# Longer rows for the split weights: eight buffers at eight places modulo 256 bytes

## The chip, the cores and the metric

The kernel runs on one core of a Trainium2 chip. The metric is the device time of one execution in microseconds (us), lower is better. The core has the engines PE (TensorE, the matrix unit; its weight loads are listed apart as PEld), ACT (ScalarE), DVE (VectorE), POOL (GpSimd) and SP (SyncE, used here to issue DMAs). SBUF is the on-chip memory with 128 partitions; a "place" below is the byte address of a row within a partition, taken modulo 256.

## The reference, cut to what matters

One layer of a hybrid decoder trunk on 512 tokens plus 16 meta tokens, 1024 channels wide, in float32:

```python
u = rmsnorm(h, mix_norm_w[i])
proj = u @ w_in[i]
...
y_pool = pool_mixer(u_pool, pool_w_group[i], pool_scale[i]) @ w_pool_up[i]
y_ssd = mamba2_branch(z, xbc, dt_raw, ...) @ w_ssd_out[i]
h = h + (gate_pool * y_pool + gate_ssd * y_ssd) @ w_o[i]
v = rmsnorm(h, mlp_norm_w[i])
hid = jax.nn.relu(v @ w_ff1[i])
h = h + (hid * hid) @ w_ff2[i]
...
out = rmsnorm(h, final_norm_w)
return out[:, N_META:]
```

Nearly all of the work is matrix products with weights that are read once from DRAM.

## The kernel before, in words

Each float32 factor of a large product is split into a high part (type fp32r, a copy by ACT) and a low part (what is left, a subtraction by DVE). A product then takes three matmuls: high by high, high by low, low by high. The weights come in 171 blocks of 128 partitions by 1024 columns, in the order of use, each by one DMA on SP's queue.

The buffers. The pool `wp` (L55) holds three raw buffers (tag `raw`), four buffers for high parts (tag `whi`) and four for low parts (tag `wlo`), each with rows of 4096 bytes, used in turn. `block_tiles` (L63) takes one of each kind; `block_part` (L70) issues the DMA, the cast `whi<-raw` (L73) and the subtraction `wlo<-raw,whi` (L74). `split` (L713) does the same from a tile that is already there (L717, L718, names `shi` and `slo`), and takes its buffers from the same tags. Tiles begin at multiples of 32 bytes. In the program as built the raw buffers begin at bytes 14816, 18912 and 23008, the high ones at 27104, 31200, 35296 and 39392, the low ones at 43488, 47584, 51680 and 55776: all eleven at place 224 modulo 256. The pool of the normed input follows: a pad of 64 bytes (`u_pad`, L124), then `uh` and `ul` (L125, L126) with rows of 2304 bytes, of which the 16 meta tokens begin at place 224 and the 512 others at place 32. Most other fp32r tiles (`yh`, `yl`, `vh`, `vl`, `hh`, `hl`, the factors of the output projection) begin at place 224 too; the pooled parts `ph`, `pl` begin at 32. The matrix of ones `ones_r` (L97), stationary at L486 and L487, begins at 128.

Who reads the split weights, and how. A matmul has a stationary operand (loaded by PEld, 128 columns of 512 bytes) and a moving one (streamed through, up to 512 columns).

- `proj_step` (L139; matmuls at L143, L144, L146): the weights are stationary, the input moves: `uh` or `ul`. In the "wide" form (`px`, `pp`) the 528 tokens go in two runs of 264, 260 or 258 columns, so places 224 and 0, or 0 and 16, or 16 and 24; in the "narrow" form (`pz`, `pgp`, `pgs`) 512 columns begin at place 32. High weights go twice (with `uh`, `ul`), low ones once.
- `mm3` (L88; L90, L91, L92): the weights are stationary, `yh`/`yl`, `yph`/`ypl` or `vh`/`vl` move, 512 columns at place 224 (tiles `pso`, `psp`, `psl`, `pup`, `pf`), or `ph`/`pl` at place 32 (`pg`).
- `wo_prod` (L771 to L773), `prod` (L956 to L958) and the last chunk (L1057): here the split weights move, 512 columns (256 at the very end), and the other factor (`hh`, `hl` and the like) is stationary. In each group of three the moving row is high, low, high.

A column slice of a block begins a multiple of 512 bytes into its row, so it has the place of its row. The order of the work is the order in which the program is written, per engine; waits come from the tile framework, by tile. `weave` (L503) interleaves the steps of two generators.

Of the kernel before, what the change touches and what calls it, by code (L numbers as in the profile page):

```python
# [10 lines left out]
F32R = mybir.dt.float32r  # L11
# [3 lines left out]
P = 128  # L15
# [34 lines left out]
def kernel(ctx: ExitStack, tc, xT, x, w, vec, fnw, out):  # L50
# [4 lines left out]
    wp = ctx.enter_context(tc.tile_pool(name="wp", bufs=4, side="left"))  # L55
# [4 lines left out]

    nblk = [0]

    def block_tiles():  # L63
        b = nblk[0]
        nblk[0] += 1
        return (b, wp.tile([P, 1024], F32, tag="raw", name=f"raw{b}", bufs=3),
                wp.tile([P, 1024], F32R, tag="whi", name=f"whi{b}"),
                wp.tile([P, 1024], F32R, tag="wlo", name=f"wlo{b}"))

    def block_part(t, c):  # L70
        b, raw, hi, lo = t
# [4 lines left out]
    def block():  # L76
        t = block_tiles()
        block_part(t, slice(0, 1024))
        return t[2:]
# [98 lines left out]
    runsB, viewB = wide(pB)  # L178

    wdt, wB = block_tiles(), block_tiles()  # L180
    b, raw, hi, lo = wdt
    nc.sync.dma_start(raw[:, :256], w[b, :, :256])
# [528 lines left out]
        woq[name, i] = t  # L711

    def split(src):  # L713
        hi = wp.tile([P, 1024], F32R, tag="whi", name=f"shi{nsplit[0]}")
        lo = wp.tile([P, 1024], F32R, tag="wlo", name=f"slo{nsplit[0]}")
        nsplit[0] += 1
        act.copy(hi, src)  # L717
        dve.tensor_tensor(lo, src, hi.bitcast(F32), op=ALU.subtract)  # L718
        return hi, lo

    nsplit = [0]
# [7 lines left out]
    for n, d in enumerate(MERGE):  # L729
        if n < len(WO_ORDER):  # L730
            wo_load(*WO_ORDER[n])
        if n + 1 < NK:
            gts.append(gate_ssd(MERGE[n + 1]))
        if n >= NK - 2:
            first.append(split(woq["b11", n - NK + 2]))
        ps = psum2(f"pup{d}")[:, :SEQ]
        wh, wl = block()
        for i, k in enumerate(ks):
            c = slice(k * P, (k + 1) * P)
            mm3(ps, (wh[:, c], wl[:, c]), yps[k], i == 0, i == NK - 1)  # L740
        dve.tensor_tensor(acc[d], acc[d], gts[n], op=ALU.mult)
        dve.tensor_tensor(m1[d], m1[d], ps, op=ALU.mult)
        dve.tensor_tensor(acc[d], acc[d], m1[d], op=ALU.add)
        factors(d)
# [70 lines left out]
    def wo_split(name):  # L815
        return [split(woq[name, i]) for i in range(2)]
# [186 lines left out]
    for c in range(NC - 1):  # L1003
        b11, b12, b22, b21 = (quarter(n) for n in ("b11_", "b12_", "b22_", "b21_"))
        z, e = c == 0, c == NC - 2
        prod(av, c, A11, split(b11), True, False)
        onto(0, 0, alpha, ADD)
        t1 = sum_of(b11, b12, "", b11)
        t2 = sum_of(t1, b22, f"t2_{c}")
        filler()  # L1010
        prod(av, c, S2, split(t2), False, False)
        onto(0, 1, alpha, SUB)
        filler()
        prod(av, c, S3, split(sum_of(b12, b22, "", b12)), False, False)
        onto(1, 1, alpha, SUB)
        filler()
        prod(av, c, A22, split(sum_of(t2, b21, "", t2)), False, True)
        onto(1, 0, alpha, ADD)
        if e:
            prod(q5v, c, S1, split(t1), z, True)  # L1020
            for t in range(2):
                onto(0, 1, q5v[t], ADD, t)
                onto(1, 1, q5v[t], ADD, t)
        elif c < NC - 3:
            filler()
        prod(av, c, S4, split(b22), True, True)
        onto(0, 1, alpha, ADD)
        prod(p2v, c, A12, split(b21), z, False)
        if not e:
            prod(q5v, c, S1, split(t1), z, False)  # L1030
# [9 lines left out]
    for t in range(4):  # L1040
        T, st = t // 2, slice((t % 2) * P, (t % 2 + 1) * P)
        n = 0
        for half in range(2):
            parts = [(0, 512)] if half == 0 or t < 3 else [(0, 256), (256, 256)]
            for a, m in parts:
# [4 lines left out]
                for k, seg in ((1, (A11, 3)[T]), (0, (A12, A22)[T])):  # L1050
                    wh, wl = wq[k, half]
                    for p in range(2):
                        x0 = p * 512 + a
                        f = i == 0 and not (T == 0 and half == 0)
# [152 lines left out]
```

## Time and profile before

| | |
|---|---|
| time, median of 2 runs | 1025.45 us (1025.28 to 1025.62) |
| span of the profiled execution, first to last instruction | 1023.3 us |
| what the median has beside that span | 2.15 us |
| granted TensorE clock, mean | 0.999 |

The page gives no other time for the profiled execution than its span, so the profile's numbers are put against 1023.3 us, and 2.15 us are added to reach the median. In a group's row "xcount | busy, mean ns of one" the mean of a matmul is its length from start to end; matmuls overlap, so the next one starts long before that. What a matmul costs is read from the distance between the starts of successive rows of the timeline.

### The profile page before, as it was taken

The numbers are of one execution on the slowest core, as the hardware profiler recorded it, in microseconds if no ns is written. First come the engines' busy times: TensorE is split into PE (matmuls) and PEld (weight loads), VectorE is DVE, ScalarE is ACT, GpSimd is POOL, SyncE is SP. The second block draws the span as 40 slices with busy tenths as digits, with TensorE's granted clock in tenths as the row PEclk, the third lists the DMA queues.
The fourth block names the chain that finished last, engine by engine and source line by source line (L and its number), as shares of the span: only waits on it lengthen the run. The fifth ranks groups of instructions, "written<-read, shape, count | busy, mean of one in ns | idle before, by whom it ended". The sixth has DMA issues, their size and how long they took to land.

```text
span 1023.3 us, 14063 instructions
## 1 busy us (share of the span) xinstructions
PE 1014.6 (99%) x5697; PEld 876.7 (86%) x5697; DVE 730.3 (71%) x954; ACT 552.5 (54%) x728; POOL 88.7 (9%) x52
## 2 busy tenths in 40 slices
PE   9999999999999999999999999999999999999997
PEld 8889989998879898988899888888888888888886
DVE  7978788687746586978755457975777577666866
ACT  7775968586627339573244343474545355454444
POOL 0100000000000000000000001003040421413400
PEclk9999999999999999999999999999999999999999
DMA  7243051414332331414532333224323323334112
GB/s 237 72 160 103 21 166 38 148 46 141 102 101 86 103 104 42 145 41 141 189 102 84 103 104 120 86 91 156 103 69 122 120 83 113 95 102 124 42 42 83
DMA packets 29281, 105.63 MB, mean 103 GB/s; under 512 B 3296, under 2 KB 4256, under 8 KB 28192
## 3 DMA queue, kind: packets, MB, share of 16 engines
q1 hardware_dynamic: 26496, 92.75, 28.7%
q0 software_dynamic: 2000, 11.08, 3.0%
q8 instruction: 45, 0.74, 0.3%
q10 hardware_dynamic: 720, 0.91, 0.3%
q14 instruction: 20, 0.16, 0.1%
HBM read 102.55 MB, written 2.16 MB: 102 GB/s over the span
## 4 chain that ended last, share of the span: by engine, by line
PE 96%; DVE 2%; ACT 0%; DMA 0%; issue 0%; SPq 0%; ACTq 0%
PE px L143 6%; PE px L144 6%; PE pf L92 6%; PE pf L91 6%; PE px L146 6%; PE pf L90 6%; PE alpha L956 3%; PE alpha L957 3%; PE alpha L958 3%; PE pz L143 3%; PE pz L146 3%; PE pz L144 3%; PE py L470 2%; PE pso L90 2%; PE pp L144 2%; PE pp L146 2%
## 5 line engine op out<-in xcount | busy, mean ns | idle before, releaser
L73 ACT CAST whi<-raw 128x1024 fp32r<-128x1024 f32 (+1 forms) x131 | 135.7, 1043 | 220.0 <-PE pf L91 55.8
L74 DVE TENSOR_TENSOR wlo<-raw,whi 128x1024 fp32r<-128x1024 f32 (+1 forms) x131 | 163.6, 1251 | 112.6 <-ACT whi L73 105.3
L143 PE MATMUL px<-uh,whi 128*128 128x264 f32 (+1 forms) x448 | 121.2, 290 | 0.7 <-DVE ct L334 0.7
L144 PE MATMUL px<-ul,whi 128*128 128x264 f32 (+1 forms) x448 | 118.9, 285 | 0.0
L90 PE MATMUL pf<-vh,whi 128*128 128x512 f32 x256 | 99.8, 390 | 0.0
L92 PE MATMUL pf<-vh,wlo 128*128 128x512 f32 x256 | 99.6, 389 | 0.0
L91 PE MATMUL pf<-vl,whi 128*128 128x512 f32 x256 | 99.6, 389 | 0.0
L146 PE MATMUL px<-uh,wlo 128*128 128x264 f32 (+1 forms) x448 | 90.8, 284 | 0.0
L143 PEld LDWEIGHTS px<-uh,whi 128*128 128x128 f32 x448 | 84.6, 189 | 2.8 <-issue 2.6
L144 PEld LDWEIGHTS px<-ul,whi 128*128 128x128 f32 x448 | 84.8, 189 | 0.3
L718 DVE TENSOR_TENSOR slo<-b,shi 128x1024 fp32r<-128x1024 f32 x35 | 49.1, 1403 | 31.6 <-ACT shi L717 31.6
L146 PEld LDWEIGHTS px<-uh,wlo 128*128 128x128 f32 x448 | 69.4, 188 | 0.3 <-issue 0.3
L717 ACT CAST shi<-b 128x1024 fp32r<-128x1024 f32 x35 | 36.8, 1050 | 47.2 <-PE pf L91 36.4
L91 PEld LDWEIGHTS pf<-vl,whi 128*128 128x128 f32 x256 | 48.1, 188 | 10.0
L90 PEld LDWEIGHTS pf<-vh,whi 128*128 128x128 f32 x256 | 48.1, 188 | 9.9
L92 PEld LDWEIGHTS pf<-vh,wlo 128*128 128x128 f32 x256 | 48.1, 188 | 9.9
L967 POOL TENSOR_TENSOR b<-b,b 128x1024 f32<-128x1024 f32 x14 | 35.7, 2548 | 238.3 <-DVE slo L718 238.3
L956 PE MATMUL alpha<-shi,hh 128*128 128x512 f32 x140 | 54.6, 390 | 0.0
L957 PE MATMUL alpha<-slo,hh 128*128 128x512 f32 x140 | 54.5, 389 | 0.0
L958 PE MATMUL alpha<-shi,hl 128*128 128x512 f32 x140 | 54.5, 389 | 0.0
L783 DVE TENSOR_TENSOR ht<-ht,alpha 128x1024 f32<-128x1024 f32 x35 | 42.5, 1214 | 10.9 <-PE alpha L958 10.9
L143 PE MATMUL pz<-uh,whi 128*128 128x512 f32 x112 | 44.0, 393 | 0.0
(412 smaller groups left out, 2513.7 us busy)
## 6 DMA issues: line engine op xcount, KB each, us to landing
raw<-in_w SPq DMA_DIRECT2D x129, 512.0 KB, 3.6
b<-in_w SPq DMA_DIRECT2D x28, 512.0 KB, 3.6
abc<-acs_d POOLq DMA_DIRECT2D x8, 1024.0 KB, 7.2
wob<-in_w SPq DMA_DIRECT2D x8, 512.0 KB, 4.6
xt<-in_xT SPq DMA_DIRECT2D x8, 264.0 KB, 5.6
ht<-in_x POOLq DMA_DIRECT2D x4, 512.0 KB, 6.7
w<-in_w SPq DMA_DIRECT2D x4, 512.0 KB, 3.6
out_dram<-out SPq DMA_DIRECT2D x4, 320.0 KB, 2.4
```

What stands on the lines that cost most here:

```text
L73: act.copy(hi[:, c], raw[:, c])
L74: dve.tensor_tensor(lo[:, c], raw[:, c], hi[:, c].bitcast(F32), op=ALU.subtract)
L90: pe.matmul(ps, ah, bh, start=first, stop=False)
L91: pe.matmul(ps, ah, bl, start=False, stop=False)
L92: pe.matmul(ps, al, bh, start=False, stop=last)
L143: pe.matmul(o, wh, rhs[0][k][:, c], start=k == 0, stop=False)
L144: pe.matmul(o, wh, rhs[1][k][:, c], start=False, stop=False)
L146: pe.matmul(o, wl, rhs[0][k][:, c], start=False, stop=k == NK - 1)
L718: dve.tensor_tensor(lo, src, hi.bitcast(F32), op=ALU.subtract)
L956: pe.matmul(ps[t], a[0], wh[:, cs], start=f, stop=False, skip_group_check=True)
L957: pe.matmul(ps[t], a[0], wl[:, cs], start=False, stop=False, skip_group_check=True)
L958: pe.matmul(ps[t], a[1], wh[:, cs], start=False, stop=l, skip_group_check=True)
```

## The change

Each high and low buffer is allocated with 1032 columns instead of 1024, 4128 bytes instead of 4096, and the first 1024 are used. 4128 is 16 times 256 plus 32, so each next buffer begins 32 bytes further on modulo 256: the four high ones at places 224, 0, 32 and 64, the four low ones at 96, 128, 160 and 192. The raw buffers stay. Everything that is allocated behind these eight moves up by 8 times 32, which is 256 bytes, and keeps its place. A high buffer and the low buffer of the same block differ by 128 bytes in place.

```diff
+    def half_tile(tag, name):
+        return wp.tile([P, 1024 + 8], F32R, tag=tag, name=name)[:, :1024]
+
     def block_tiles():
         b = nblk[0]
         nblk[0] += 1
         return (b, wp.tile([P, 1024], F32, tag="raw", name=f"raw{b}", bufs=3),
-                wp.tile([P, 1024], F32R, tag="whi", name=f"whi{b}"),
-                wp.tile([P, 1024], F32R, tag="wlo", name=f"wlo{b}"))
+                half_tile("whi", f"whi{b}"), half_tile("wlo", f"wlo{b}"))
...
     def split(src):
-        hi = wp.tile([P, 1024], F32R, tag="whi", name=f"shi{nsplit[0]}")
-        lo = wp.tile([P, 1024], F32R, tag="wlo", name=f"slo{nsplit[0]}")
+        hi = half_tile("whi", f"shi{nsplit[0]}")
+        lo = half_tile("wlo", f"slo{nsplit[0]}")
```

## The prediction

> **What bounds the kernel now.** I read the page first: its head, the slices, the chain that ended last.
>
> ```profile
> span 1023.3 us, 14063 instructions
> PE 1014.6 (99%) x5697; PEld 876.7 (86%) x5697; DVE 730.3 (71%) x954; ACT 552.5 (54%) x728; POOL 88.7 (9%) x52
> PEclk9999999999999999999999999999999999999999
> PE 96%; DVE 2%; ACT 0%; DMA 0%; issue 0%; SPq 0%; ACTq 0%
> ```
>
> PE is busy for 99% of the span at the full granted clock and is 96% of the chain. So the time is the sum of the distances between starts of successive matmuls, and little else. The engines that write the buffers whose rows get longer come next, from the groups by line:
>
> ```profile
> L73 ACT CAST whi<-raw 128x1024 fp32r<-128x1024 f32 (+1 forms) x131 | 135.7, 1043 | 220.0 <-PE pf L91 55.8
> L74 DVE TENSOR_TENSOR wlo<-raw,whi 128x1024 fp32r<-128x1024 f32 (+1 forms) x131 | 163.6, 1251 | 112.6 <-ACT whi L73 105.3
> ```
>
> The cast waits for PE to free a buffer (L91 and others), not PE for the cast: the weights arrive ahead of their use.
>
> What one matmul costs depends on its form, and here the timeline of PE is read, first rows and last rows of undisturbed stretches. First 512 columns whose moving row begins at place 224: six rows of the product with the squared hidden layer, then the next projection.
>
> ```profile
> 786.76 0.39 PE L956 MATMUL alpha<-shi,hh 128*128 128x512 f32 x1
> 786.99 0.39 PE L957 MATMUL alpha<-slo,hh 128*128 128x512 f32 x1
> 787.22 0.39 PE L958 MATMUL alpha<-shi,hl 128*128 128x512 f32 x1
> ...
> 793.11 0.39 PE L91 MATMUL pf<-vl,whi 128*128 128x512 f32 x1
> 793.34 0.39 PE L92 MATMUL pf<-vh,wlo 128*128 128x512 f32 x1
> 793.56 0.39 PE L956 MATMUL alpha<-shi,hh 128*128 128x512 f32 x1
> ```
>
> From 786.76 to 793.56 there are 30 distances: 226.7 ns each, the same in `alpha`, where split weights move, and in `pf`, where they are stationary. Now 512 columns at place 32, a narrow projection between two products `pup` at 224:
>
> ```profile
> 585.04 0.40 PE L143 MATMUL pgs<-uh,whi 128*128 128x512 f32 x1
> ...
> 585.74 0.39 PE L143 MATMUL pgs<-uh,whi 128*128 128x512 f32 x1
> ...
> 590.32 0.39 PE L146 MATMUL pgs<-uh,wlo 128*128 128x512 f32 x1
> 590.55 0.40 PE L90 MATMUL pup<-yph,whi 128*128 128x512 f32 x1
> ...
> 592.86 0.39 PE L91 MATMUL pup<-ypl,whi 128*128 128x512 f32 x1
> ...
> 595.81 0.39 PE L92 MATMUL pup<-yph,wlo 128*128 128x512 f32 x1
> ```
>
> The projection settles: 585.74 to 590.55 is 21 distances of 229.0 ns, so place 32 costs 2.3 ns more than place 224. The first three take 233 ns each (0.70 us), 4 more. Behind the change of place back to 224 the first ten take 231 ns each (2.31 us), and only then, from 592.86 to 595.81, the 13 distances are 226.9. So the place of a moving row is seen in the time, and after a change PE needs up to ten matmuls to get back into its best step. That is the whole stage on which this change acts.
>
> **The change, part by part.** It adds no instruction, no DMA and no wait, and moves none past another. It moves addresses. Four things can come of that.
>
> 1. The cast and the subtraction write rows at other places. They do the same work; I price that at nothing. The cover is the wait quoted above (ACT idle 220.0 us ahead of L73). If each became a tenth dearer, some 105 ns a cast, PE would still not wait, except for the first blocks; ACT has 0% of the chain and DVE 2%, so a tenth of all of DVE's share, about 2 us, is a bound that lies far above.
>
> 2. The split weights as moving rows, 864 matmuls: 588 at L956 to L958, 168 at L771 to L773, 108 at L1057. Counted from these groups and their smaller ones:
>
> ```profile
> L956 PE MATMUL alpha<-shi,hh 128*128 128x512 f32 x140 | 54.6, 390 | 0.0
> L957 PE MATMUL alpha<-slo,hh 128*128 128x512 f32 x140 | 54.5, 389 | 0.0
> L958 PE MATMUL alpha<-shi,hl 128*128 128x512 f32 x140 | 54.5, 389 | 0.0
> ```
>
> They now begin at place 224 without exception; afterwards one buffer in eight does, so 756 matmuls are moved off it. The price of another place is known from one row, place 32: +2.3 ns. Bounds: at the least -6.7 ns (worked out under the third rival), at the most +4.3 ns, what the unsettled rows behind the change of place show. I take +2.3, the one settled value: 756 x 2.3 = 1.7 us.
>
> 3. In these 864 the place also changes within each group of three (high, low, high: two changes, 128 bytes apart), 576 changes. What does a change cost when it comes steadily? The wide projections change place four times in six matmuls. These rows are 264 columns at 224 and 0 in turn, and 258 columns at 16 and 24:
>
> ```profile
> 113.32 0.28 PE L143 MATMUL px<-uh,whi 128*128 128x264 f32 x1
> ...
> 116.99 0.28 PE L143 MATMUL px<-uh,whi 128*128 128x264 f32 x1
> 121.46 0.28 PE L143 MATMUL px<-uh,whi 128*128 128x258 f32 x1
> ...
> 124.34 0.28 PE L143 MATMUL px<-uh,whi 128*128 128x258 f32 x1
> ```
>
> 30 distances of 122.3 and 24 of 120.0 ns. From 258 to 512 columns at 226.7 is 0.42 ns a column; by that 264 columns would be 122.5 with no change of place at all. So the steady change costs nothing here. The other end is the change into `pgs`: three distances together 0.70 us instead of 0.687, 13 to 16 ns a change, 576 x 16 = 9.2 us. I take 1.5 ns, near the rows that alternate steadily as these will: 0.9 us.
>
> 4. The split weights as stationary operand: 4128 matmuls (L90 to L92 464 each, L143 to L146 912 each), whose weight rows now come from eight places. All of them begin at 224 now, but the sums over heads load a matrix of ones from place 128:
>
> ```profile
> L486 PEld LDWEIGHTS png<-qhg,ones_r 128*128 128x128 f32 x8 | 1.5, 188 | 0.3
> L90 PEld LDWEIGHTS pf<-vh,whi 128*128 128x128 f32 x256 | 48.1, 188 | 9.9
> ```
>
> 188 ns from both, and the load lies beside the matmul ahead of it. I take zero for the place of a stationary row, with eight loads as evidence. The upper bound is the first rival, the lower one the fourth.
>
> **Weighed against the skill.** The rows above say that the moving row's place counts. The Trainium skill (SBUF — State Buffer, "Who interferes with whom") says that PE has two read ports, one for the moving operand and one for LDWEIGHTS, independent of each other, and that "PE and ACT never wait on anyone". The equal 188 ns agree with it; the 229.0 against 226.7 ns show that a place has a price all the same. By that page alone, the change would be worth zero, which is the second rival.
>
> Sum: 1.7 + 0.9 = 2.6 us on the span of 1023.3, so 1025.9. The median has 2.15 us beside the span (1025.45 less 1023.3), which nothing here touches: 1028.0 us.
>
> **The rivals.**
>
> First, the step is lost everywhere. If the distance hangs on how the moving and the stationary row lie to each other, then high and low weights that differ by 128 bytes change that relation inside each group of three, and PE stays in the unsettled state: 231 ns instead of 226.7 for the 512-column matmuls at 224 (1344 with stationary weights and the 864 above), 231 instead of 229.0 for 816 at place 32, and perhaps 1 ns for 1920 wide ones. 2208 x 4.3 + 816 x 2.0 + 1.9 us = 13.0 us, so 1038.5. For it: the unsettled rows exist and last ten matmuls although nothing waits. Against it: the equal load times, and the steady alternation at 120.0 ns.
>
> Second, nothing happens: the place matters only in `uh`-like rows, or settles by itself: 1025.4 us. For it: 256, 258, 264 columns lie on one line. Against it: 229.0 ns at place 32, also for another tensor.
>
> Third, a little faster. The distance may grow in steps: 258 columns take 120.0, and the last products, of 256 columns at place 224, take the same, 20 distances in 2.40 us:
>
> ```profile
> 1014.69 0.28 PE L1057 MATMUL pl<-shi,hh 128*128 128x256 f32 x1
> ...
> 1017.09 0.28 PE L1057 MATMUL last<-shi,hl 128*128 128x256 f32 x1
> ```
>
> If a step is 16 columns (6.7 ns at 0.42 each) and a row that begins at a multiple of 64 bytes saves one, half of the 864 gain: 432 x -6.7 = -2.9, the other places +0.7, so about 1023.2 us. Against it: no row here shows place 0, 64, 128 or 192 with 512 columns.
>
> Fourth, far faster. At 0.42 ns a column 512 columns are worth 215.1 ns; 11.6 ns of each distance are left over. If half of that were a clash of equal places and went, 4992 x 5.8 = 29 us, 996 us. The Trainium skill (TensorE: Matmul & The Clock Gate, "Back-to-back issue gap") gives N/2.4 + 2.5, an estimate of 216 ns for 512, as what can be reached; the trace has 226.7. Against this rival: 258 columns at 16 and 24, clear of the weights' place, have the same surplus.
>
> Fifth, slower by more than 2%: some of the new pairs of places cost PE one whole step of 6.7 ns in every matmul, at all 4992 of fp32r with split weights: 33 us, 1059 us. It decides from 4.1 ns a matmul on (20.5 us over 4992). For it: place 32 costs something at each matmul. Against it: even the unsettled rows average only 4.3 ns over the best.
>
> **How the numbers follow.** Forecast 0.46 (1028.0; its own range 1025 to 1036, by the bounds of terms 2 and 3), step lost everywhere 0.24 (1038.5), nothing 0.13 (1025.4), a little faster 0.10 (1023.2), slower by over 2% 0.05, far faster 0.02. For eight in ten I leave out the far cases and the dear end of the first rival: 1022.5 to 1040. Two per cent is 20.5 us, and the chances go by that although the two runs shown lie within 0.4 us of each other, so that a smaller difference can be told too: faster 0.02, same 0.93, slower 0.05.
>
> **What would show it.** Timeline of PE in the changed kernel: `pf` rows still 226.7 apart, `pgs` 229.0 and `px` 122.3 (term 4 right); `alpha` rows on average some 3 ns further apart, differing from buffer to buffer (terms 2 and 3). If `pf` rows lie 229 to 232 apart, the first rival holds; if `alpha` rows from some buffers are 220 apart, the third. Casts and subtractions stay at 1043 and 1251 ns. The forecast falls if the place of a stationary row has a price: it is the term with the most matmuls and the thinnest evidence.

## The result and the profile after

The changed kernel takes 1037.46 us (1037.43 to 1037.49, 2 runs) against 1025.45 before: ratio 1.0118, interval 1.0089 to 1.0147, slower by 12.0 us. That lies inside the range on record, and beside its number: 1038.5 was the first rival, 1028.0 the forecast. It is under the two per cent (20.5 us) from which the prediction speaks of slower, but far more than the 0.4 us between the two runs of the kernel before.

The page of the changed kernel (two lines were added ahead of all matmuls, so L90 is now L92, L143 is L145 and L956 is L958):

```profile
span 1035.4 us, 14063 instructions
PE 1027.2 (99%) x5697; PEld 878.5 (85%) x5697; DVE 730.0 (71%) x954; ACT 553.0 (53%) x728; POOL 88.9 (9%) x52
PEclk9999999999999999999999999999999999999999
PE 99%; DVE 1%; ACT 0%; issue 0%; ACTq 0%
L75 ACT CAST whi<-raw 128x1024 fp32r<-128x1024 f32 (+1 forms) x131 | 135.4, 1040 | 226.3 <-PE pf L93 58.2
L76 DVE TENSOR_TENSOR wlo<-raw,whi 128x1024 fp32r<-128x1024 f32 (+1 forms) x131 | 163.1, 1247 | 116.9 <-ACT whi L75 116.9
```

The span grew by 12.1 us and PE's busy time by 12.6, with the same number of matmuls at the same clock. Casts and subtractions kept their length (1040 and 1247 ns, before 1043 and 1251), and ACT waits longer for PE than before. No wait was added: PE takes longer over the same list.

The timeline of PE shows where, at the same matmuls as before. First the six of `alpha` and the 24 of `pf`; then a narrow projection (its high weights at place 64) and the product `pup` behind it; then the wide runs:

```profile
793.91 0.39 PE L958 MATMUL alpha<-shi,hh 128*128 128x512 f32 x1
...
800.87 0.40 PE L958 MATMUL alpha<-shi,hh 128*128 128x512 f32 x1
588.99 0.40 PE L145 MATMUL pgs<-uh,whi 128*128 128x512 f32 x1
...
593.89 0.39 PE L92 MATMUL pup<-yph,whi 128*128 128x512 f32 x1
...
599.22 0.40 PE L94 MATMUL pup<-yph,wlo 128*128 128x512 f32 x1
113.74 0.29 PE L145 MATMUL px<-uh,whi 128*128 128x264 f32 x1
...
117.39 0.28 PE L145 MATMUL px<-uh,whi 128*128 128x264 f32 x1
121.86 0.28 PE L145 MATMUL px<-uh,whi 128*128 128x258 f32 x1
...
124.76 0.28 PE L145 MATMUL px<-uh,whi 128*128 128x258 f32 x1
```

30 distances from 793.91 take 232.0 ns each (before 226.7), 21 from 588.99 take 233.3 (229.0), the 23 of `pup` 231.7, and there is no settled stretch at 226.9 behind its tenth row any more. The wide runs barely move: 121.7 and 120.8 ns (122.3 and 120.0).

Both traces hold the same matmuls in the same order, so every distance can be set against its own. Added up by use, the differences are:

| matmuls | count | longer by, us |
|---|---|---|
| stationary weights, moving row at 224 (`pf`, `pso`, `psp`, `psl`, `pup`) | 1344 | 6.0 |
| split weights moving (`alpha` and its like, `wo_prod`, last chunk) | 864 | 4.1 |
| stationary weights, moving row at 32 (narrow, `pg`) | 816 | 2.2 |
| stationary weights, wide | 1920 | -0.1 |
| all others | 753 | -0.1 |

Two thirds of the loss (6.0 and 2.2 us) sit where the moving rows stayed at the same place and only the stationary ones went elsewhere.

### The profile page after: what moved, and what is told of

Read it like the earlier page. It is cut to its first block, busy times and chain, and to the rows that moved or that the text cites. A ratio compares the mean times of both kernels' runs of the same rounds, so it can differ in the third digit from the quotient of the medians.

```text
span 1035.4 us, 14063 instructions
## 1 busy us (share of the span) xinstructions
PE 1027.2 (99%) x5697; PEld 878.5 (85%) x5697; DVE 730.0 (71%) x954; ACT 553.0 (53%) x728; POOL 88.9 (9%) x52
## 4 chain that ended last, share of the span: by engine, by line
PE 99%; DVE 1%; ACT 0%; issue 0%; ACTq 0%
PE px L145 6%; PE px L148 6%; PE px L146 6%; PE pf L94 6%; PE pf L92 6%; PE pf L93 6%; PE alpha L960 3%; PE alpha L958 3%; PE alpha L959 3%; PE pz L148 3%; PE pz L146 3%; PE pz L145 3%; PE py L472 2%; PE pso L92 2%; PE pp L148 1%; PE pp L145 1%
## 5 line engine op out<-in xcount | busy, mean ns | idle before, releaser
L75 ACT CAST whi<-raw 128x1024 fp32r<-128x1024 f32 (+1 forms) x131 | 135.4, 1040 | 226.3 <-PE pf L93 58.2
L76 DVE TENSOR_TENSOR wlo<-raw,whi 128x1024 fp32r<-128x1024 f32 (+1 forms) x131 | 163.1, 1247 | 116.9 <-ACT whi L75 116.9
L145 PE MATMUL px<-uh,whi 128*128 128x264 f32 (+1 forms) x448 | 121.2, 291 | 0.7 <-DVE ct L336 0.7
L92 PE MATMUL pf<-vh,whi 128*128 128x512 f32 x256 | 101.0, 395 | 0.0
L145 PEld LDWEIGHTS px<-uh,whi 128*128 128x128 f32 x448 | 84.5, 189 | 2.8 <-issue 2.6
L92 PEld LDWEIGHTS pf<-vh,whi 128*128 128x128 f32 x256 | 48.3, 189 | 10.8
L958 PE MATMUL alpha<-shi,hh 128*128 128x512 f32 x140 | 55.3, 395 | 0.0
L148 PE MATMUL pz<-uh,wlo 128*128 128x512 f32 x112 | 44.3, 395 | 0.0
```

What stands on the lines that cost most here:

```text
L75: act.copy(hi[:, c], raw[:, c])
L76: dve.tensor_tensor(lo[:, c], raw[:, c], hi[:, c].bitcast(F32), op=ALU.subtract)
L92: pe.matmul(ps, ah, bh, start=first, stop=False)
L145: pe.matmul(o, wh, rhs[0][k][:, c], start=k == 0, stop=False)
L148: pe.matmul(o, wl, rhs[0][k][:, c], start=False, stop=k == NK - 1)
L958: pe.matmul(ps[t], a[0], wh[:, cs], start=f, stop=False, skip_group_check=True)
```

## The experiments

Two theories were set against each other. R, the relation: the distance between matmuls depends on the place of the moving row less that of the stationary row, modulo 256. A, the alternation: what costs is that high and low weights of one group of three lie 128 bytes apart, which keeps PE from settling. All runs start from the kernel before; padding is written as tiles that nothing uses, always 256 bytes in all (512 with four places), so that what lies behind keeps its place. In the diffs, `...` stands for lines left out.

**All eight buffers at place 32.**

```diff
...
+        raw = wp.tile([P, 1024], F32, tag="raw", name=f"raw{b}", bufs=3)
+        if b == 0:
+            wp.tile([P, 16], F32, tag="pad1", name="pad1", bufs=1)
+        hi = wp.tile([P, 1024], F32R, tag="whi", name=f"whi{b}")
+        lo = wp.tile([P, 1024], F32R, tag="wlo", name=f"wlo{b}")
+        if b == 0:
+            wp.tile([P, 48], F32, tag="pad3", name="pad3", bufs=1)
...
```

> All eight split buffers at one place, 32 instead of 224 (64 bytes of padding ahead of them, 192 behind). Theory R (relation: the distance between matmuls depends on how the stationary row lies to the moving row): the narrow projections pgs, whose moving row is at 32 too, fall from 229.0 to 226.7 ns; alpha, moving at 32 against stationary 224, rises to 229.0 as pgs has before; pf, moving 224 against stationary 32, leaves 226.7 for something between 228 and 232. Time 1025.5 - 1.9 (816 x 2.3 ns) + 2.0 (864 x 2.3) + 1.7 to 6.7 (1344 x 1.3 to 5) = 1027 to 1032 us. Theory A (alternation: what costs is that high and low weights of one group of three lie 128 bytes apart): no alternation here, so pf stays at 226.7, pgs at 229.0, and only alpha pays its moving place: 1027.5 us.

Measured: 1033.12 us (1032.78 to 1033.23), ratio 1.0077 (1.0062 to 1.0092). The timeline, first a narrow projection and `pup` behind it, then a block of `pf`:

```profile
585.03 0.40 PE L148 MATMUL pgs<-uh,whi 128*128 128x512 f32 x1
...
589.80 0.39 PE L95 MATMUL pup<-yph,whi 128*128 128x512 f32 x1
...
595.17 0.39 PE L97 MATMUL pup<-yph,wlo 128*128 128x512 f32 x1
791.24 0.39 PE L95 MATMUL pf<-vh,whi 128*128 128x512 f32 x1
...
796.84 0.40 PE L961 MATMUL alpha<-shi,hh 128*128 128x512 f32 x1
```

The projection is at 227.1 ns over 21 distances with its first ones still unsettled (229.0 before), and `pup` and `pf`, whose operands have now different places, at 233.5 and 233.3. The best and the dear distances changed sides with the weights, though high and low lie at one place. A gives `pf` 226.7 and falls short. R had the signs right and the price of `pf` too low (233.3, not 228 to 232), and the time is 1 us above its range. For `alpha`, now at difference 64, it had 229.0 ns; over the whole run the `alpha` rows average 231.3.

**High ones at 224, low ones at 96.** The padding of 128 bytes stands between `hi` and `lo`, another 128 behind.

```diff
...
+            wp.tile([P, 32], F32, tag="pad2", name="pad2", bufs=1)
+        lo = wp.tile([P, 1024], F32R, tag="wlo", name=f"wlo{b}")
...
+            wp.tile([P, 32], F32, tag="pad3", name="pad3", bufs=1)
...
```

> All four high buffers at 224, all four low ones at 96: the 128 bytes of the change inside each group, but nothing differs from buffer to buffer. Theory A: the whole loss, pf and alpha at 231 to 232 ns, 1035 to 1038 us. Theory R: only the matmuls around the low weights are off their best relation, a third of them; pf and alpha at 227 to 230 ns, 1028 to 1033 us.

Measured: 1033.89 us (1033.73 to 1034.39), ratio 1.0085 (1.0069 to 1.0102), between the two.

```profile
792.17 0.39 PE L961 MATMUL alpha<-shi,hh 128*128 128x512 f32 x1
...
793.54 0.39 PE L95 MATMUL pf<-vh,whi 128*128 128x512 f32 x1
...
799.09 0.39 PE L961 MATMUL alpha<-shi,hh 128*128 128x512 f32 x1
```

`alpha` takes 228.3 ns in these six, `pf` 231.3 in these 24: the first as R had it, the second as A had it. Averaged line by line over all rows of the run, the starts say more. Of the three matmuls of an `alpha` group only the one with the low weights is dear (234.0 ns; 227.1 and 226.2 for the two with high ones). In `pf` two of three are: the one with the low weights (234.2) and the one ahead of it (232.5), against 226.7 for the third. In `alpha` the place changes twice in a group, but only the matmul that lies off its stationary row pays; that speaks for R, while the totals of this run decide nothing by themselves.

**Rows of 4128 bytes, each low buffer at the place of its high one.**

```diff
...
+        hi = wp.tile([P, 1032], F32R, tag="whi", name=f"whi{b}")[:, :1024]
...
+            wp.tile([P, 32], F32, tag="pad2", name="pad2", bufs=1)
+        lo = wp.tile([P, 1032], F32R, tag="wlo", name=f"wlo{b}")[:, :1024]
...
+            wp.tile([P, 32], F32, tag="pad3", name="pad3", bufs=1)
...
```

`split` takes rows of 1032 columns in the same way.

> Rows of 4128 bytes as in the change, but each low buffer at the same place as its high one: four places (224, 0, 32, 64), no difference inside a group of three. Theory A: pf settles at 226.7 ns in every block, 1025.5 to 1028 us. Theory R: pf keeps 226.7 in the blocks at 224 alone, the other three of four lie at 229 to 232: 1030 to 1036 us.

Measured: 1036.22 us (1036.03 to 1036.47), ratio 1.0108 (1.0092 to 1.0123). The first rows of three blocks of `pf` one after the other, from buffers at places 0, 224 and 64, and the row behind them:

```profile
708.07 0.40 PE L95 MATMUL pf<-vh,whi 128*128 128x512 f32 x1
...
713.67 0.39 PE L95 MATMUL pf<-vh,whi 128*128 128x512 f32 x1
...
719.12 0.39 PE L95 MATMUL pf<-vh,whi 128*128 128x512 f32 x1
...
724.73 0.39 PE L961 MATMUL alpha<-shi,hh 128*128 128x512 f32 x1
```

24 distances each: 233.3, 227.1 and 233.8 ns. Only the block whose weights lie where the moving row lies is fast, its neighbours are not, and nothing alternates inside a group. Without the alternation, the loss is still 11 us of the change's 12. A is refuted as the main cause. R again priced too low: it had 229 to 232 ns for the dear blocks, and the time is 0.2 us above its range.

The same run has `alpha` from buffers at place 64 and at place 0, which gives two differences that no other run holds steadily, 96 and 32:

```profile
766.42 0.40 PE L961 MATMUL alpha<-shi,hh 128*128 128x512 f32 x1
...
769.23 0.39 PE L95 MATMUL pf<-vh,whi 128*128 128x512 f32 x1
774.83 0.40 PE L961 MATMUL alpha<-shi,hh 128*128 128x512 f32 x1
...
777.63 0.39 PE L95 MATMUL pf<-vh,whi 128*128 128x512 f32 x1
```

12 distances each: 234.2 and 233.3 ns.

**High rows of 4352 bytes, every place kept.**

```diff
...
-                wp.tile([P, 1024], F32R, tag="whi", name=f"whi{b}"),
+                wp.tile([P, 1088], F32R, tag="whi", name=f"whi{b}")[:, :1024],
...
-        hi = wp.tile([P, 1024], F32R, tag="whi", name=f"shi{nsplit[0]}")
+        hi = wp.tile([P, 1088], F32R, tag="whi", name=f"shi{nsplit[0]}")[:, :1024]
...
```

> High rows of 4352 bytes, so that every buffer keeps place 224: a check that the length of a row and the shift of what lies behind it cost nothing by themselves. Theories R and A both: 1025.5 us, all distances as before. A theory that the row length or a coarser alignment (512 bytes and more) counts: 1028 us or more.

Measured: 1025.07 us (1024.65 to 1025.87), ratio 0.9999 (0.9990 to 1.0008). Longer rows, slices instead of whole tiles and a shift by 1024 bytes of all that follows cost nothing. With every place modulo 256 kept, there is no loss.

**The input moved to the weights.** If R holds, the kernel before has something to gain: its narrow projections have the moving row at 32, the weights at 224.

```diff
-    up.tile([P, 16], F32, name="u_pad")
     uh = [up.tile([P, 64 + SEQ], F32R, name=f"uh{k}")[:, 64 - NM :] for k in range(NK)]
     ul = [up.tile([P, 64 + SEQ], F32R, name=f"ul{k}")[:, 64 - NM :] for k in range(NK)]
+    up.tile([P, 16], F32, name="u_pad")
```

> The kernel before, with the 64 bytes of padding behind the tiles uh and ul instead of ahead of them: their 512 tokens then begin at place 224, where the weights are, and the wide runs at 160 and 192. The weights are not touched. Theory R (what counts is the place of the moving row less that of the stationary one): pgs, pz and pgp fall from 228.9 to 226.7 ns (648 x -2.2 = -1.4 us); the wide runs then lie to the weights (-64 and -32) as they did in the kernel with all weights at 32, where they took 121.3 and 119.2 ns instead of 122.0 and 120.0 (1728 x -0.75 = -1.3 us): about 1022.5 us, faster than the kernel before. If instead the weights' own place counts, or the moving row's alone: no change at pgs or at px, 1024 to 1025.5 us.

Measured: 1022.03 us (1021.55 to 1022.54), ratio 0.9971 (0.9960 to 0.9982): faster than the kernel before by 3.0 us. Narrow projection and wide runs:

```profile
583.50 0.39 PE L143 MATMUL pgs<-uh,whi 128*128 128x512 f32 x1
...
588.26 0.39 PE L90 MATMUL pup<-yph,whi 128*128 128x512 f32 x1
113.31 0.28 PE L143 MATMUL px<-uh,whi 128*128 128x264 f32 x1
...
116.95 0.28 PE L143 MATMUL px<-uh,whi 128*128 128x264 f32 x1
121.40 0.28 PE L143 MATMUL px<-uh,whi 128*128 128x258 f32 x1
...
124.26 0.28 PE L143 MATMUL px<-uh,whi 128*128 128x258 f32 x1
```

226.7 ns for the narrow ones (21 distances), 121.3 and 119.2 for the wide ones: the numbers that the run with all weights at 32 had led to expect, reached from the other side, with the weights where they were. Taken alone, this run could also be read as place 224 being good for any moving row, as the prediction had it (the expectation wrongly gave that reading no change). The run with all weights at 32 rules that out: there the narrow projection fell to 227.1 ns with its moving row still at 32, and `pf` rose to 233.3 with its moving row still at 224. So it is the difference of two places, not either place.

**The first stage's input as well.** The edit ahead, and 48 columns ahead of `xh`, 40 behind `xl` instead of 24.

```diff
...
+    pre.tile([P, 48], F32, name="x_pad0")
...
-    pre.tile([P, 24], F32, name="x_pad")
+    pre.tile([P, 40], F32, name="x_pad")
...
```

> The same, and xh and xl of the first stage shifted by 192 bytes too, so that their 512 tokens begin at 224. Theory R: 120 narrow matmuls at -2.2 ns and 192 wide ones at -0.75 more, -0.4 us: about 1022.1 us. Otherwise as for the run with uh and ul alone.

Measured: 1021.86 us (1021.58 to 1022.23), ratio 0.9969 (0.9958 to 0.9981). It is the fastest of all versions by its median, but not to be told from the one ahead of it.

**All eight at 160, all eight at 96.** Two more differences, by the padding of the first run, in other sizes (at 160; for 96 both are 32 columns).

```diff
...
+            wp.tile([P, 48], F32, tag="pad1", name="pad1", bufs=1)
...
+            wp.tile([P, 16], F32, tag="pad3", name="pad3", bufs=1)
...
```

> All eight weight buffers at 160. Theory R: pf (224 less 160 is +64, as pgs had it before) at 228.9 ns, alpha (160 less 224 is -64, as pf had it with all weights at 32) at 233.3; pgs at 32 less 160, -128, not seen steadily so far: 229 to 233. Time 1025.3 + 3.0 (1344 x 2.2) + 5.6 (864 x 6.5) + 0 to 3.6, wide runs +-1.9: 1032 to 1039 us. If the sign of the difference did not count, pf and alpha would both be at 229.

> All eight at 96. Theory R: pgs (32 less 96, -64) at 233.3 ns (816 x 4.3 = +3.5 us); pf (+128) and alpha (-128) the same as each other, since 128 and -128 are one place modulo 256, and not below 229: 2208 x 2.3 to 6.6 = 5 to 14.6 us. 1034 to 1043 us.

Measured: 1036.16 us (1035.74 to 1036.81), ratio 1.0110 (1.0094 to 1.0125), and 1041.54 us (1041.37 to 1041.70), ratio 1.0162 (1.0148 to 1.0176); both inside what R expected. With weights at 160, six rows of `alpha` and two blocks of `pf`:

```profile
777.08 0.40 PE L95 MATMUL pf<-vh,whi 128*128 128x512 f32 x1
...
782.59 0.39 PE L961 MATMUL alpha<-shi,hh 128*128 128x512 f32 x1
785.39 0.40 PE L95 MATMUL pf<-vh,whi 128*128 128x512 f32 x1
...
790.99 0.39 PE L961 MATMUL alpha<-shi,hh 128*128 128x512 f32 x1
792.39 0.40 PE L961 MATMUL alpha<-shi,hh 128*128 128x512 f32 x1
...
793.79 0.40 PE L95 MATMUL pf<-vh,whi 128*128 128x512 f32 x1
```

`alpha` (-64, so 192) takes 233.3 ns. `pf` (+64) takes 229.6 in one block and 233.3 in the other, which R alone did not say (it had 228.9): blocks at this difference settle at one of two values. With weights at 96:

```profile
591.53 0.39 PE L148 MATMUL pgs<-uh,whi 128*128 128x512 f32 x1
...
596.43 0.39 PE L95 MATMUL pup<-yph,whi 128*128 128x512 f32 x1
798.36 0.40 PE L95 MATMUL pf<-vh,whi 128*128 128x512 f32 x1
...
803.96 0.40 PE L961 MATMUL alpha<-shi,hh 128*128 128x512 f32 x1
```

The narrow ones (-64) are at 233.3 over 21 distances and `pf` (+128) at 233.3 over 24.

The differences with 512 columns together, from the rows shown here and in the prediction:

| moving less stationary, modulo 256 | ns between starts | seen in |
|---|---|---|
| 0 | 226.7 | `pf`, `alpha` before; `pgs` with the input moved |
| 32, 96 | 233.3, 234.2 | `alpha`, pairs at 0 and at 64 |
| 64 | 229.0 or 233.3 | `pgs` before; `pf` with weights at 160 |
| 128 | 233.3 | `pf` with weights at 96 |
| 160, 224 | 233.8, 233.3 | `pf`, pairs at 64 and at 0 |
| 192 | 233.3 | `pf`, weights at 32; `pgs`, weights at 96 |

## Why the prediction was right and wrong

The range held because it had been drawn wide enough to take in the first rival. The sum behind the forecast did not hold: 1037.46 us is 9.5 us above its 1028.0 and outside its own range of 1025 to 1036, and most of the loss came from a term that it put at zero. That the time lies in the range on record is owed to the rival, not to the forecast's mechanism.

The bound was read rightly: PE's distances are the time, and no other engine came into it. Step 1 (casts and subtractions at nothing) held: 1040 and 1247 ns.

Steps 2 and 3 (split weights moving, 1.7 + 0.9 = 2.6 us) measured 4.1 us, within their bounds. Two figures there do not come out. The matmuls whose moving weights leave place 224 are 728 in the program as built, not 756, since high weights go twice and some of their buffers keep it; the term stays at 1.7 us. And the bounds of the two terms, 756 x -6.7 ns = -5.1 us and 756 x 4.3 ns + 9.2 us = 12.5 us, give 1020.4 to 1037.9 us on top of 1025.45, not 1025 to 1036. The price was taken from `pgs`, the one settled place beside 224. That row was misread: its 229.0 ns are the price of the difference +64, not of place 32, as the run with the input moved and the one with all weights at 32 show, and +64, in its cheaper state, is the cheapest of the differences other than zero that were found.

Step 4 failed: the place of a stationary row was priced at zero, and it measured 8.0 us (6.0 + 2.2 - 0.1, the table by use). The evidence was eight loads from place 128 that last 188 ns like those from 224. The length of a load does not show the price. In the changed kernel the loads of the group whose matmuls got dearer still last 189 ns on the mean:

```profile
L92 PEld LDWEIGHTS pf<-vh,whi 128*128 128x128 f32 x256 | 48.3, 189 | 10.8
```

What the runs showed in its place is the first rival's condition, that the distance hangs on how the two rows lie to each other. Its price, 4.3 ns for 2208 matmuls or 9.5 us, measured 10.1 us (6.0 + 4.1); its 1.6 us for the narrow ones measured 2.2; its 1.9 us for the wide ones did not come, they are 0.1 us shorter. Its picture of PE kept unsettled by the two differences inside each group is only part of it: with pairs at one place nothing alternates, and the blocks off the moving row's place settle, at 233.3 ns.

Why was it so close to being seen? Every split weight of the kernel before lay at 224, and so did the other operand of 2208 of the matmuls with 512 columns, the difference zero, so the best case looked like the ordinary one. The transient behind each change from `pgs` to `pup`, ten matmuls at 231 ns, was quoted as the rival's evidence and given 0.24. It was in fact a stage passing from one difference to another.

The rule of the Trainium skill (SBUF — State Buffer, "Who interferes with whom") that PE has two independent read ports and never waits on anyone does not describe this case: between differences 0 and 192 lie 6.6 ns of each matmul, though the work of the other engines is the same. The time by that rule would have been 1025.4; 1037.46 was measured. The estimate of 216 ns for 512 columns by the Trainium skill (TensorE: Matmul & The Clock Gate, "Back-to-back issue gap"), which calls its formula the gap of an isolated matmul and sets about 131 ns beside it for a sustained stream, was not reached at any difference tried; 226.7 was the least.

Left open: by what mechanism the two rows meet. The load of the next stationary operand starts with the present matmul (in the run with high ones at 224 and low ones at 96, a load at 793.77 beside the `pf` matmul at 793.77, 0.19 us long), so a moving row and the next stationary row may be read at the same time. That run bears on it: in `pf` the matmul ahead of the low weights lies right to its own stationary row and not to the next one, and it takes 232.5 ns; the one with the low weights lies right to the next row and not to its own, and it takes 234.2. By this both relations seem to count, but a cost of each change from one stationary place to another would give the same two numbers, and the narrow projections of that run do not fall into line (229.8 ns for the low weights at difference 192, 233.3 and 232.0 for the high ones at 64). It was not separated further.

## What to carry to other kernels

Where PE is the bound, read the distance between starts for each form of matmul, and set it against the address of both operands modulo 256: here equal places gave 226.7 ns for 512 columns, others 229.0 to 234.2, and moving 64 bytes of padding was worth 3.0 us, ratio 0.9971 (0.9960 to 0.9982). Spreading buffers over many places is then the wrong remedy: it puts most pairs off the good difference; for rows of 512 columns, line the moving rows up with the stationary ones. And a duration that does not change (188 ns of a load) is no evidence that the work beside it is not held up.

## What was not expected of the hardware

At difference +64 blocks of the same form settle at 229.6 or at 233.3 ns (weights at 160, above); what decides between the two was not found.

Short rows want another difference than long ones, as far as one stretch in each of two kernels shows it. The last products, of 256 columns, take 120.0 ns with both operands at 224; with the moving weights at 160 against stationary rows at 224 the same 20 distances are 113.5 ns, while 512 columns at that difference rise to 233.3:

```profile
1025.72 0.28 PE L1062 MATMUL pl<-shi,hh 128*128 128x256 f32 x1
...
1027.99 0.28 PE L1062 MATMUL last<-shi,hl 128*128 128x256 f32 x1
```

In both cases the change is about 6.6 ns, once down and once up. The wide runs, too, were best (121.3 and 119.2 ns) with no run at difference zero.
